# Score products of the global heads: 64-row operands for the keys' low parts, two heads at a time

## The chip, the cores and the metric

The kernel runs on one core of one Trainium2 chip. The metric is the device time of one execution in microseconds (us), as the median of several runs. The engines are named as in the profile: PE is the matrix engine's multiplying, PEld its loading of stationary operands ("weights"), DVE is VectorE, ACT is ScalarE, POOL is GpSimd, SP issues most of the transfers.

## The reference, cut to what matters

A two-layer encoder trunk on 1024 tokens of width 1024. Layer 0 projects its normalised input into three groups of heads and a gate; the group that matters here is the first, global attention with 8 query heads that share 2 key and value heads, of 64 channels each, every query against all 1024 keys:

```python
qa = rope_2d(rmsnorm(qa.reshape(B, S, A_HEADS, HEAD_DIM), q_norm_a[e]), grid_row, grid_col)
ka = rope_2d(rmsnorm(ka.reshape(B, S, A_KV, HEAD_DIM), k_norm_a[e]), grid_row, grid_col)
ya = global_gqa(qa, ka, va.reshape(B, S, A_KV, HEAD_DIM))
...
s = jnp.einsum('bqkgd,bskd->bkgqs', qblk, k).astype(jnp.float32) * scale
p = jax.nn.softmax(s, axis=-1).astype(v.dtype)
return jnp.einsum('bkgqs,bskd->bqkgd', p, v)
```

After it come windowed attention, attention over 256 memory tokens, a gate, an output projection, and layer 1 (neighbourhood attention). The change touches only the global attention of layer 0.

## The kernel before, in words

**Numbers in two parts.** Matrix products run on a 32-bit type that is multiplied at reduced precision (F32R). So nearly every operand is held as a high part and a low part (the value less its high part), and a product is the sum of high by high, high by low and low by high.

**Layout of the global heads.** Four pairs of heads (`even`, L1916, `for j in range(4)`), each done by one call of `global_pair` (L1024). For head `i` of a pair the tile `qs[i]` is 128 partitions by 1024 queries: the 64 rows from `64*i` on hold the queries' high parts, the other 64 rows their low parts (written so by `q_unit`, L917). The key tiles `kh` and `kl` hold the 64 channels of one key head twice, once on each half of the partitions: `kh` the high parts, `kl` the low parts. One 128-row product of `qs[i]` with `kh` thus gives high by high and low by high together; a second one, with `kl`, gives high by low, and low by low as well.

**One score** (`scores(i, g, b)`, L1030) takes one head `i` and 128 queries, block `2*g + b`. Four matrix products, each 128 rows by 128 queries by 512 keys, go to a PSUM tile `sa` of 128 by 1024 (two banks; there are two such tiles): for either half of the keys one with `kh` (L1035), then one with `kl` (L1036). DVE takes the maximum (L1040), ACT the exponential and its sum (L1041), DVE the reciprocal (L1042), POOL scales the result in the tile `P` (L1043). 16 scores make a pair; the order is all blocks of head 0, then all of head 1.

**Turning and multiplying.** For each head and each `g`, two blocks `P` are turned in 128 by 128 pieces (`flip`, L133), four to a PSUM tile `tr`; `p_parts` splits the result into a high part (ACT, L125) and a low part (DVE, L542), and each part is multiplied with the values `v` (L1068, 256 columns a product), over all keys, into the tile `o`. The values' high and low parts give the upper and the lower 64 rows of `o`; ACT copies the lower ones (`bt`, L1073), DVE adds the upper ones and writes 64 rows by 256 queries of the pair's output `y` (L1074).

**Work put between.** Projections of later tiles (gates, memory queries) are lists of steps of three 512-column products each (`token_steps`, L242). `pull(n)` issues `n` of them, and `issue_after` keeps them behind the newest score product or turn (`self.fence`). `global_pair` pulls 4 after each of its first two scores, then one at each pair of key blocks. Likewise one step of `side`, which makes sums of the output weights on POOL (`weight_sums`, L1246), follows each later score.

**What sets the order.** The program is written in this order and then put in another one by a scheduler that runs the instructions on a timeline of its own (`TC`, L52); the numbers of `AHEAD["l0"]` (L37) move a kind of instruction forward: `score` by 20, `exp` by 60, `part` by 150, `close` by 120. Each engine then runs its instructions in that fixed order.

**Buffers around it.** Tag `q` has 4 tiles, `P` 6, the PSUM tiles `sa` 2, `tr` 2, `o` 1. The `q` tiles of the next pair are loaded by L1021, and these can start only when the last score that reads a tile is done. After `global_pair`, `gated_rows` multiplies the whole `y` with its gate, and `mem_att` (L615) uses the `sa` tiles too.

Of the kernel before, what the change touches and what calls it, by code (L numbers as in the profile page):

```python
# [12 lines left out]
AF = mybir.ActivationFunctionType  # L13
OP = mybir.AluOpType
AX = mybir.AxisListType
# [3 lines left out]
T = 1024  # L19
# [45 lines left out]
class Trunk:  # L65
# [958 lines left out]
    def global_pair(self, qs, ks, v, kv, y, side):  # L1024

        nc = self.nc
        kh, kl = ks
        pts = {}

        def scores(i, g, b):  # L1030
            qb = qs[i][:, (2 * g + b) * 128:(2 * g + b + 1) * 128]
            s = self.ps("sa", (128, T))
            with self.ahead("score"):
                for c in range(0, T, 512):
                    nc.tensor.matmul(s[:, c:c + 512], qb, kh[:, c:c + 512], start=True, stop=False)  # L1035
                    self.fence = nc.tensor.matmul(s[:, c:c + 512], qb, kl[:, c:c + 512], start=False, stop=True)  # L1036
            st = self.tiny()
            pt = self.st("P", [128, T])
            with self.ahead("exp"):
                nc.vector.tensor_reduce(st[:, 0:1], s, axis=AX.X, op=OP.max, negate=True)  # L1040
                nc.scalar.activation(pt, s, AF.Exp, bias=st[:, 0:1], accum_out=st[:, 1:2])  # L1041
                nc.vector.reciprocal(st[:, 2:3], st[:, 1:2])  # L1042
                self.normal = nc.gpsimd.tensor_scalar(pt, pt, st[:, 2:3], 0.5, op0=OP.mult, op1=OP.mult)  # L1043
            pts[i, g, b] = pt

        todo = [(i, g, b) for i in range(2) for g in range(4) for b in range(2)]
        for _ in range(2):
            scores(*todo.pop(0))
            self.pull(4)
        for i in range(2):  # L1050
            for g in range(4):
                p = [pts[i, g, b] for b in range(2)]
                o = self.ps("pv")
                for c in range(0, 8, 2):
                    if c in (0, 4) and todo:
                        scores(*todo.pop(0))
                        with self.tc.issue_after(self.normal.ins):
                            next(side, None)
                    tr = self.ps("tr")
                    with self.ahead("flip"):  # L1060
                        self.flip((tr[:, (2 * k + b) * 128:(2 * k + b + 1) * 128],
                                   p[b][:, (c + k) * 128:(c + k + 1) * 128]) for k in range(2) for b in range(2))
                    parts = self.p_parts(tr, 512)
                    self.pull(1)
                    with self.ahead("pv"):
                        for k in range(2):
                            for part in parts:
                                nc.tensor.matmul(o[:, :256], v[:, c + k, kv, :], part[:, k * 256:(k + 1) * 256],  # L1068
                                                 start=(c + k == 0 and part is parts[0]),
                                                 stop=(c + k == 7 and part is parts[1]))  # L1070
                bt = self.st("bt", [64, 512])
                with self.ahead("close"):
                    self.copy(bt[:, :256], o[64:128, :256])  # L1073
                    nc.vector.tensor_tensor(y[64 * i:64 * i + 64, g * 256:(g + 1) * 256], o[0:64, :256], bt[:, :256],  # L1074
                                            op=OP.add)

# [1148 lines left out]
```

## Time and profile before

| what | value |
|---|---|
| median of 3 runs | 1484.51 us (1483.56 to 1491.91) |
| the profiled execution, its own time | 1488.39 us |
| its span, first to last instruction | 1486.6 us |
| share of the span in which PE, PEld, DVE, ACT, POOL were busy | 99%, 86%, 70%, 56%, 43% |
| first and last score product of the global heads | 144.3 us, 447.8 us |
| last output of the global heads (L1074) | 480.4 us |

The rows of a timeline give the start, the time taken, the engine, the line, the operation, output and inputs by tile names, the array's rows and columns that it uses ("128\*128"), and partitions by columns. Matrix products are pipelined: a product of 512 columns "takes" 0.39 us while the next one starts well before that is over, so the pace of PE is read from the starts and not from the durations. The table of groups has, behind the operation, the count, busy time, the mean of one in ns, and the idle time before it.

### The profile page before, as it was taken

What the parts mean: (1) busy time and instruction counts of PE and PEld (TensorE: products, weight loads), DVE (VectorE), ACT (ScalarE), POOL (GpSimd) and SP (SyncE); (2) the same over time, 40 slices, a digit from 0 to 9 for tenths busy, and PEclk for the clock granted to TensorE, in tenths of its full rate; (3) what the DMA queues carried; (4) which work ended last, traced back from release to release, by engine and by line L of the source; (5) the groups of instructions that cost most, each with busy time, mean ns of one, the idle gap of its engine ahead of it and who ended that gap; (6) DMA issues with size and microseconds to landing.
All of it is one profiled execution on the core that took longest, in us unless ns stands there. A gap on an engine that the chain in (4) does not pass through costs nothing.

```text
span 1486.6 us, 25518 instructions
## 1 busy us (share of the span) xinstructions
PE 1465.6 (99%) x8433; PEld 1275.1 (86%) x8433; DVE 1034.8 (70%) x2124; ACT 837.9 (56%) x1877; POOL 642.2 (43%) x767
## 2 busy tenths in 40 slices
PE   9899999999999999999999999999999999999998
PEld 8798888988888788888879887888998888888886
DVE  6687777777776578776687776654446787778674
ACT  7743665556655366655444444444446777777454
POOL 1223568556765656553450000001425556664454
PEclk9999999999999999999999999999999999999999
DMA  8966334334343524378553343567665568788834
GB/s 286 306 159 183 118 119 162 114 128 137 115 139 106 172 76 141 106 265 310 185 181 128 128 140 136 157 169 245 229 245 173 187 195 272 235 287 316 315 107 144
DMA packets 173860, 271.92 MB, mean 183 GB/s; under 512 B 15648, under 2 KB 96800, under 8 KB 172704
## 3 DMA queue, kind: packets, MB, share of 16 engines
q1 hardware_dynamic: 173296, 270.20, 56.2%
q8 instruction: 67, 1.10, 0.3%
q14 instruction: 65, 0.53, 0.1%
q10 hardware_dynamic: 432, 0.09, 0.0%
HBM read 174.28 MB, written 83.89 MB: 174 GB/s over the span
## 4 chain that ended last, share of the span: by engine, by line
PE 85%; DMA 5%; DVE 4%; issue 2%; ACT 2%; POOL 2%; SPq 0%; POOLq 0%; DVEq 0%; ACTq 0%
PE pj L242 15%; PE pj L62 11%; PE x L1619 7%; PE tr L133 6%; PE pv L1068 4%; PE y L1619 4%; PE pv L62 3%; PE s L62 3%; PE pj L1334 3%; PE tr L62 3%; PE sa L1334 2%; PE pv L1619 2%; PE sa L1035 2%; PE sa L1036 2%; PE s L1334 2%
## 5 line engine op out<-in xcount | busy, mean ns | idle before, releaser
L542 DVE TENSOR_TENSOR pl<-tr,ph 128x512 fp32r<-128x512 f32 (+2 forms) x352 | 204.1, 594 | 45.0 <-ACT ph L125 43.0
L242 PE MATMUL pj<-H,wh 128*128 128x512 f32 x704 | 233.7, 412 | 0.5 <-DVE vt L313 0.2
L125 ACT ACTIVATE ph<-tr 128x512 fp32r<-128x512 f32 (+2 forms) x352 | 176.3, 522 | 100.5 <-PE tr L133 76.4
L158 POOL TENSOR_SCALAR wh<-wraw 128x512 fp32r<-128x512 f32 x48 | 32.6, 682 | 275.9 <-PE x L1619 234.0
L125 ACT ACTIVATE wh<-wraw 128x384 fp32r<-128x384 f32 (+1 forms) x163 | 89.0, 553 | 99.4 <-DMA wraw<-w_mem 12.9
L242 PE MATMUL pj<-H,wl 128*128 128x512 f32 x352 | 139.1, 395 | 0.0
L242 PEld LDWEIGHTS pj<-H,wh 128*128 128x128 f32 x704 | 120.2, 189 | 18.3 <-POOL wh L158 1.1
L62 PE MATMUL pj<-H,wh 128*128 128x512 f32 x384 | 121.0, 396 | 0.0
L1121 POOL TENSOR_SCALAR pn<-pn,st 128x384 f32<-128x384 f32 (+1 forms) x128 | 72.4, 567 | 104.7 <-DVE st L1120 69.0
L133 PE MATMUL tr<-ident,P 128*128 128x128 f32 x752 | 115.4, 273 | 0.7 <-DVE pl L542 0.4
L1281 POOL TENSOR_TENSOR wl<-wraw,wh 128x384 fp32r<-128x384 f32 x56 | 63.2, 1130 | 91.4 <-ACT wh L125 85.6
L1119 ACT ACTIVATE pn<-pn,st 128x384 f32<-128x384 f32 (+1 forms) x128 | 75.1, 587 | 42.2 <-DVE st L1116 41.0
L133 PEld LDWEIGHTS tr<-ident,P 128*128 128x128 f32 x752 | 88.9, 140 | 9.1 <-DVE pl L542 1.4
L1041 ACT ACTIVATE P<-sa,st 128x1024 f32<-128x1024 f32 x64 | 71.5, 1117 | 35.3 <-PE tr L133 19.1
L1043 POOL TENSOR_SCALAR P<-P,st 128x1024 f32<-128x1024 f32 x64 | 74.0, 1159 | 32.3 <-DVE st L1042 32.3
L1040 DVE TENSOR_REDUCE st<-sa 128x1 f32<-128x1024 f32 x64 | 77.5, 1219 | 8.3 <-PE sa L1036 7.9
L62 PE MATMUL s<-k,q 128*128 128x384 f32 (+1 forms) x352 | 81.2, 327 | 0.0
L242 PEld LDWEIGHTS pj<-H,wl 128*128 128x128 f32 x352 | 66.2, 188 | 15.3
L62 PE MATMUL pj<-H,wl 128*128 128x512 f32 x192 | 75.6, 394 | 0.0
L160 POOL TENSOR_TENSOR wl<-wraw,wh 128x512 fp32r<-128x512 f32 x52 | 68.7, 1324 | 10.9 <-ACT wh L125 8.4
L62 PEld LDWEIGHTS pj<-H,wh 128*128 128x128 f32 x384 | 66.6, 188 | 5.4
L853 PE MATMUL pj<-ah,H 128*128 128x256 f32 x384 | 70.5, 281 | 0.0
(569 smaller groups left out, 4187.1 us busy)
## 6 DMA issues: line engine op xcount, KB each, us to landing
wraw<-w_o SPq DMA_DIRECT2D x52, 256.0 KB, 4.1
y<-yb SPq DMA_DIRECT2D x24, 512.0 KB, 3.2
wraw<-s SPq DMA_DIRECT2D x64, 192.0 KB, 3.7
wraw<-w_e SPq DMA_DIRECT2D x44, 256.0 KB, 3.2
k<-k SPq DMA_DIRECT2D x42, 256.0 KB, 5.4
s<-bias SPq DMA_DIRECT2D x56, 192.0 KB, 2.0
wq<-w_o SPq DMA_DIRECT2D x40, 256.0 KB, 3.4
y<-sg SPq DMA_DIRECT2D x18, 512.0 KB, 3.3
```

The costliest lines, as they stand in the source:

```text
L62: return lambda *a, **k: self.tc.keep_in_program_order(getattr(self.engine, name)(*a, **k))
L125: return self.nc.scalar.activation(out, in_, AF.Copy, scale=scale)
L133: self.turned = self.fence = self.pe.transpose(o, i, self.ident)
L242: self.pe.matmul(a[:, :n], s[:, kt % UNIT, :], m, start=(kt == 0 and i == 0), stop=(kt == KT - 1 and i == 2))
L542: self.low = nc.vector.tensor_tensor(pl[:, :n], tr[:, :n], ph[:, :n], op=OP.subtract)
L1040: nc.vector.tensor_reduce(st[:, 0:1], s, axis=AX.X, op=OP.max, negate=True)
L1041: nc.scalar.activation(pt, s, AF.Exp, bias=st[:, 0:1], accum_out=st[:, 1:2])
L1043: self.normal = nc.gpsimd.tensor_scalar(pt, pt, st[:, 2:3], 0.5, op0=OP.mult, op1=OP.mult)
L1119: nc.scalar.activation(o, o, AF.Exp, bias=st[:, 0:1], scale=-1.0, accum_out=st[:, 2:3])
L1121: self.normal = normal = nc.gpsimd.tensor_scalar(o, o, st[:, 3:4], 0.5, op0=OP.mult, op1=OP.mult)
L1334: last = nc.tensor.matmul(bank, s[:, k, :], y[3 * u + k][m][:, cols], start=start and u + k + e == 0, stop=u == 1 and k + e == 4, skip_gro ...
L1619: self.last = nc.tensor.matmul(bank, ws[s][:, k, :], b[k][m], start=start and k + i == 0, stop=k == UNIT - 1 and i == 2, skip_group_check= ...
```

## The change

The loop over scores of one head becomes a loop over blocks of queries, with both heads of the pair at once. For a block it takes both `sa` tiles and issues, in a fixed order (each product behind the one before it): four 128-row products with `kh` (head 1, then head 0, two halves of the keys each), then four products with `kl`, each of which uses only the 64 rows of the queries' high parts: rows 64 to 127 for head 1, rows 0 to 63 for head 0, in turn. The low-by-low part of the scores is no longer formed. The softmax of head 0 is written behind the products, that of head 1 two key-block pairs later (where before the next score stood). Turning and multiplying take the two heads of one block side by side, where they took two blocks of one head; the output's last addition, 64 rows by 256 queries, becomes two of 128 queries each, one for either head.

```diff
-        def scores(i, g, b):
-            qb = qs[i][:, (2 * g + b) * 128:(2 * g + b + 1) * 128]
-            s = self.ps("sa", (128, T))
+        def product(s, q, k, c, start):
+            with self.tc.issue_after(self.fence.ins) if self.fence else nullcontext():
+                self.fence = nc.tensor.matmul(s[:, c:c + 512], q, k[:, c:c + 512], start=start, stop=not start)
+
+        def scores(g, b):
+            qb = [q[:, (2 * g + b) * 128:(2 * g + b + 1) * 128] for q in qs]
+            ss = [self.ps("sa", (128, T)) for _ in range(2)]
             with self.ahead("score"):
+                self.fence = None
+                for i in (1, 0):
+                    for c in range(0, T, 512):
+                        product(ss[i], qb[i], kh, c, True)
                 for c in range(0, T, 512):
-                    nc.tensor.matmul(s[:, c:c + 512], qb, kh[:, c:c + 512], start=True, stop=False)
-                    self.fence = nc.tensor.matmul(s[:, c:c + 512], qb, kl[:, c:c + 512], start=False, stop=True)
...
+                    for i in (1, 0):
+                        r = slice(64 * i, 64 * i + 64)
+                        product(ss[i], qb[i][r], kl[r], c, False)
+            for i, s in enumerate(ss):
...
+                pts[i, g, b] = pt
+                yield
+
+        def sided():
+            with self.tc.issue_after(self.normal.ins):
+                next(side, None)
+        todo = [(g, b) for g in range(4) for b in range(2)]
+        for _ in scores(*todo[0]):
             self.pull(4)
...
+        for n, (g, b) in enumerate(todo):
+            p = [pts[i, g, b] for i in range(2)]
+            o = self.ps("pv")
+            later = scores(*todo[n + 1]) if n + 1 < len(todo) else None
+            for c in range(0, 8, 2):
+                if c in (0, 4) and later:
+                    next(later)
+                    sided()
...
+                for i in range(2):
+                    nc.vector.tensor_tensor(y[64 * i:64 * i + 64, (2 * g + b) * 128:(2 * g + b + 1) * 128],
+                                            o[0:64, i * 128:(i + 1) * 128], bt[:, i * 128:(i + 1) * 128], op=OP.add)
```

More of the change, by code (lines that the diff above doesn't have):

```diff
@@ L1033, in scores @@
             with self.ahead("score"):
+                self.fence = None
+                for i in (1, 0):
+                    for c in range(0, T, 512):
+                        product(ss[i], qb[i], kh, c, True)
                 for c in range(0, T, 512):
-                    nc.tensor.matmul(s[:, c:c + 512], qb, kh[:, c:c + 512], start=True, stop=False)
-                    self.fence = nc.tensor.matmul(s[:, c:c + 512], qb, kl[:, c:c + 512], start=False, stop=True)
-            st = self.tiny()
@@ L1038, in scores @@
[L1038 to L1046, printed above, removed]
@@ L1047, in global_pair @@
-        for _ in range(2):
-            scores(*todo.pop(0))
-            self.pull(4)
[L1050 to L1075, printed above, removed]
```

22 lines of the change are left out of this document (added).

## The prediction

> **What bounds the kernel now.** I read the page first: PE is busy in 99% of the span, so the question is what PE pays for. Then the busy time by stretches from 140 to 460 us, in which all score products of the global heads lie (only the first and the last stretch and the sum are shown; the columns are the engines' busy us and counts, then the granted clock, the DMA share and GB/s), and the waits of PE in the same window.
>
> ```profile
> span 1486.6 us, 25518 instructions
> PE 1465.6 (99%) x8433; PEld 1275.1 (86%) x8433; DVE 1034.8 (70%) x2124; ACT 837.9 (56%) x1877; POOL 642.2 (43%) x767
> ```
> ```profile
> 140.00:180.00 40.00, 39.91 (x221) 33.92 (x220) 28.95 (x45) 22.93 (x40) 27.96 (x31) 1.00 0.44 128
> ...
> 420.00:460.00 40.00, 40.00 (x261) 36.00 (x261) 30.36 (x49) 22.60 (x44) 27.18 (x35) 1.00 0.37 111
> sum 320.00, PE 319.52 PEld 280.52 DVE 234.59 ACT 190.38 POOL 209.31; mean PE 39.94 PEld 35.06 DVE 29.32 ACT 23.80 POOL 26.16
> ```
> ```profile
> PE tr L133 <- DVE pl L542: 0.4, 1, 0.4
> ```
>
> PE works through 319.52 of 320 us, waits once for 0.4 us, and its clock is full (1.00). The next engine, DVE, is busy 234.59 us, 73%. So here a microsecond of PE is a microsecond of the kernel, until something else falls due. The chain of waits says the same, and the table of groups gives the counts:
>
> ```profile
> by line: PE pj L242 39.2%; PE tr L133 18.0%; PE pv L1068 17.1%; PE sa L1035 9.2%; PE sa L1036 9.2%; PE pv L670 2.6%; PE sa L630 1.2%; PE sa L629 1.2%; PE sa L631 1.2%; DVE sg L438 0.5%; DVE vt L313 0.2%; ACT sg L437 0.2%; DVE pl L542 0.2%;
> ```
> ```profile
> L1035 PE MATMUL sa<-k,q 128*128 128x512 f32 x128 | 51.6, 403 | 0.0
> L1036 PE MATMUL sa<-k,q 128*128 128x512 f32 x128 | 50.2, 392 | 0.0
> ```
>
> The products with the low key parts (L1036) are 9.2% of 320 us, 29.4 us. The pace of one comes from the timeline of PE in a run of them, and that of the weight loads from the same stretch of PEld:
>
> ```profile
> 252.16 0.39 PE L1035 MATMUL sa<-k,q 128*128 128x512 f32 x1
> 252.39 0.40 PE L1036 MATMUL sa<-k,q 128*128 128x512 f32 x1
> ...
> 253.32 0.39 PE L1036 MATMUL sa<-k,q 128*128 128x512 f32 x1
> 253.55 0.28 PE L1068 MATMUL pv<-ph,va 128*128 128x256 f32 x1
> ```
> ```profile
> 252.16 0.19 PEld L1036 LDWEIGHTS sa<-k,q 128*128 128x128 f32 x1
> 252.40 0.19 PEld L1035 LDWEIGHTS sa<-k,q 128*128 128x128 f32 x1
> ```
>
> From 252.16 to 253.55 there are six steps, so 0.232 us each; 128 of them are 29.7 us, which agrees with the chain. A product lives 0.39 us, 0.16 us longer than until the next one starts. The load for a product starts at the moment its predecessor starts (252.16, 252.40): PE loads one product ahead.
>
> **The change part by part.**
>
> *The paired products.* All 256 score products stay; 128 of them shrink from 128 rows to 64, and neighbours use opposite halves of the array. Every product in the trace has the form 128\*128, so no row shows whether two halves run at once. Bounds: not at all, 0; wholly, a pair in the time of one, which saves 2 x 0.232 = 0.464 us for a block of queries (four products with `kl`) and, with 32 blocks, 14.8 us. Two loads have to fit in each 0.232 us. That they can is seen where products follow faster than loads are needed here:
>
> ```profile
> 257.12 0.46 PEld L133 LDWEIGHTS tr<-ident,P 128*128 128x128 f32 x4
> 257.55 0.19 PEld L1035 LDWEIGHTS sa<-k,q 128*128 128x128 f32 x1
> 257.66 0.19 PEld L1036 LDWEIGHTS sa<-k,q 128*128 128x128 f32 x1
> ```
> ```profile
> 257.22 0.60 PE L133 MATMUL tr<-ident,P 128*128 128x128 f32 x4
> 257.58 0.47 PE L1035 MATMUL sa<-k,q 128*128 128x512 f32 x1
> 257.89 0.39 PE L1036 MATMUL sa<-k,q 128*128 128x512 f32 x1
> ```
>
> Loads start 0.11 us apart (257.55, 257.66), so two take 0.22 us. I take the pairs as running together.
>
> *The second load of a pair.* PE loads one product ahead, so at the first pair the second half's weights are loaded only once the first half runs. The rows above price a product without weights ready: from 257.58 to 257.89 are 0.31 us in place of 0.232, 0.08 us too many. From then on both halves stay offset by that much. Bounds 0 and 0.11 us (one load) a block; I take 0.08.
> The Trainium skill (TensorE: Matmul & The Clock Gate, Part 3 on packing small matmuls) gives about 4 ns between the starts of products in different row groups. By it this term is nothing and the sum below would be -7.2 us instead of -4.6; no run here shows it yet.
>
> *The two edges of a block.* PE goes from 128-row products to 64-row ones and back: 64 edges in all. The trace has no such change. Nearest below: from the turns (32-bit, 128 columns) to the products of L1035, where PE also changes what it does, only the missing load shows, 0.08 us. Bounds: 0 if the edge is free; 0.35 us if the array must empty (0.16, the life of a product beyond its successor's start) and then load in full (0.19). Between them: the empty array plus an uncovered load as the rows show it, 0.16 + 0.08 = 0.24. I take half of that, 0.12 us, since nothing in the rows says that all products must be out before the next may enter.
>
> *Sum for PE.* A block: 0.464 - 0.08 - 2 x 0.12 = 0.144 us gained; 32 blocks: 4.6 us.
>
> *Softmax of two heads at once.* The counts of L1040 to L1043 are as before. Both `sa` tiles are now filled together and both must be empty before the next block, where before one was read while the other was filled:
>
> ```profile
> L1040 DVE TENSOR_REDUCE st<-sa 128x1 f32<-128x1024 f32 x64 | 77.5, 1219 | 8.3 <-PE sa L1036 7.9
> L1042 DVE RECIPROCAL st<-st 128x1 f32<-128x1 f32 x64 | 10.1, 158 | 24.8 <-ACT P L1041 24.5
> L1074 DVE TENSOR_TENSOR yb<-pv,bt 64x256 f32<-64x256 f32 x29 | 11.9, 412 | 2.0 <-ACT bt L125 1.5
> ```
> ```profile
> L1041 ACT ACTIVATE P<-sa,st 128x1024 f32<-128x1024 f32 x64 | 71.5, 1117 | 35.3 <-PE tr L133 19.1 <-DVE st L1040 16.1
> L1041 ACT ACTIVATION_READ_ACCUMULATOR P<-sa,st 128x1 f32 x64 | 12.6, 197 | 0.0
> ```
> ```profile
> L1043 POOL TENSOR_SCALAR P<-P,st 128x1024 f32<-128x1024 f32 x64 | 74.0, 1159 | 32.3 <-DVE st L1042 32.3
> ```
>
> Two maxima, one exponential and its sum: 2 x 1.219 + 1.117 + 0.197 = 3.75 us from a block's last product until both tiles are free; with the reciprocal and the scaling 0.158 + 1.159 = 5.07 us until the second `P` is ready. Blocks are 10.5 us apart on average (336.1 us, from the first score product at 144.3 to the last output at 480.4, over 32):
>
> ```profile
> L1035 PE MATMUL sa<-k,q x128: 388/393/486, 144.3 to 447.6; 128*128 128x512 f32 x128
> ```
> ```profile
> L1074 DVE TENSOR_TENSOR yb<-pv,bt x32: 397/418/420, 165.9 to 480.4; 64x256 f32<-64x256 f32 x32
> ```
>
> Each pair's first block has 8 pulled steps of 0.70 us (172.39 to 173.09 below) behind it, 5.6 us, which covers 5.07. So I price it at nothing; what hides it is the turning, the value products and the pulled steps. Without that cover it is the third rival.
>
> *The output's addition.* 32 additions of 64x256 (0.412 us) become 64 of 64x128. Bounds: the same total, or twice, 13.2 us more on DVE. DVE would go from 73% to 77% at most; PE hides it, so nothing. On the last block of a pair the gate waits up to 0.4 us longer, with the memory attention's products on PE meanwhile.
>
> *What else moves.* Pulled steps and `side` steps are as many as before (8 and 32; 14 a pair), behind the newest score as before. Both heads' `q` tiles are now held until a pair's last block, where the first came free at half; so the two loads for the next pair, on SP's queue with the projection weights behind them, can start later than they did. The rows of their issue and landing, and of the first pair's last score and the second pair's first:
>
> ```profile
> L1021 SPq DMA_DIRECT2D q<-qa x6: 320/430/590, 166.5 to 368.4; - x6
> ...
> DMA to landing us min/median/max: 3.6/4.8/6.0
> ```
> ```profile
> 192.07 0.40 PE L1035 MATMUL sa<-k,q 128*128 128x512 f32 x1
> ```
> ```profile
> 214.29 0.39 PE L1035 MATMUL sa<-k,q 128*128 128x512 f32 x1
> ```
>
> 22 us lie between, and a load lands in 6.0 at most. Nothing.
>
> *Sum.* -4.6 us. The profiled execution took 1488.4 us, 1.8 beyond its span and 3.9 over the median; the products cost the same in each, so I subtract from the median: 1484.5 - 4.6 = **1479.9 us**.
>
> **The rivals.**
>
> *Free edges, 1469.7 us.* The halves run together, offset and edges cost nothing: the whole 14.8 us. For it: loads run one product ahead, and a change from turns to products costs no more than its load. Against it: a different use of the rows of the array is more than another operation.
>
> *The array empties at both edges, 1487.6 us: slower than before.* Place: between the last product with `kh` and the first with `kl`, and between the last with `kl` and whatever follows. Price 0.24 us each: 0.464 - 0.08 - 0.48 = -0.096 a block, +3.1 us. It decides from 0.192 us an edge on, where 0.464 - 0.08 is used up. For it: products overlap by 0.16 us and each block has two edges for only two saved steps. Against it: no row shows PE emptying itself by its own will. Should the loads not be overlapped either (0.35 us an edge, 0.11 us offset), it is +11.1 us, 1495.6.
> The Trainium skill states this rule (TensorEngine Tiling (Array Packing), Key Properties): a change of the tiling mode, unlike a change of tile, drains TensorE. Its cost in time is not given there, and no run here has shown it so far.
>
> *Both score tiles are late, 1488.9 us.* Where scores follow closely, a pair of them comes every 4.96 us:
>
> ```profile
> 170.55 0.40 PE L1035 MATMUL sa<-k,q 128*128 128x512 f32 x1
> ...
> 172.39 0.62 PE L242 MATMUL pj<-H,wh 128*128 128x512 f32 x2
> ...
> 173.09 0.40 PE L1035 MATMUL sa<-k,q 128*128 128x512 f32 x1
> ...
> 175.51 0.39 PE L1035 MATMUL sa<-k,q 128*128 128x512 f32 x1
> ```
>
> A block at that pace, 4.82 us with the gain, has 1.71 us of products (8 x 0.232 - 0.144), which leaves 3.11 us for 3.75 us of softmax: PE waits 0.64 us. Over half of the 28 later blocks that is 9.0 us, +4.4 in all; over all of them +13.3. Against it: the average distance of 10.5 us, and an order that is made with such waits in view.
>
> *The halves run one after the other, 1492.2 us.* A 64-row product then costs the same 0.232 us and the edges stay: 64 x 0.12 = +7.7 us (1506.9 at 0.35 an edge). The change would not do what it says. The trace says nothing for or against it except that loads would not stop it.
>
> **How the numbers follow.** Forecast 0.38, free edges 0.17, emptied array 0.20, late score tiles 0.15, one after the other 0.10. The range goes from 1467, the free case less 2.7 us for a luckier order of the rest (PE idles only 1486.6 - 1465.6 = 21 us in all, so there is little to win), to 1494, beyond the last rival and just short of the bound of 1495.6. The forecast's own range is 1474 to 1484. A measurement of this kernel tells about 1% from no change, 14.8 us: that is what the free case just reaches, so faster by more gets 0.11 (half of that case and a little for order), slower by more 0.08 (products in turn with full edges, or late tiles at every block), and within 1% the rest, 0.81.
>
> **What would show it.** Right: 128 products of form 64\*128 in the stage; the second of a pair starts about 0.1 us behind the first and the next pair 0.23 us after that one; 0.3 to 0.4 us instead of 0.232 from the last 128-row product to the first 64-row one, and the same on the way out; PE still at 99% and its stage some 5 us shorter. Wrong: 64-row products 0.232 us apart (one after the other); gaps of 0.45 us and more at the edges (emptied); PE idle before L1035's successors, released by ACT's exponential (late tiles); a stage 15 us shorter (free).

## The result and the profile after

The changed kernel takes 1492.87 us (median of 20 runs), the kernel before 1486.7 us (median of 20 runs, a little over the 1484.51 us of its first three). The ratio is 1.0041, with a 95% interval of 1.0031 to 1.0051: slower by 6.1 us, 4.6 to 7.6. One of the changed kernel's 20 runs took 5093 us; nothing recorded says why, and the ratio leaves it out. The forecast was 1479.9 us.

The page of the changed kernel, its span and busy times:

```profile
span 1490.8 us, 25565 instructions
PE 1467.1 (98%) x8433; PEld 1257.3 (84%) x8433; DVE 1039.8 (70%) x2156; ACT 839.6 (56%) x1877; POOL 649.0 (44%) x767
```

The table of groups by form, from 140 to 460 us of the changed kernel, score products and the output's addition (count, busy us, mean ns, idle us before):

```profile
L1032 PE MATMUL sa<-k,q 128*128 128x512 f32 x128 | 40.7, 401 | 3.5 <-ACT P L1051 3.3
L1032 PE MATMUL sa<-k,q 64*128 64x512 f32 x128 | 25.2, 446 | 0.0
```
```profile
L1087 DVE TENSOR_TENSOR yb<-pv,bt 64x128 f32<-64x128 f32 x58 | 16.2, 280 | 3.7 <-ACT bt L125 3.2
```

The change did what it says: 128 products of form 64\*128. Their busy time is 0.62 of the others' (25.2 against 40.7 us, though each lives a little longer), because two of them run at once. But PE, which before waited once for 0.4 us, now waits 3.3 us for ACT's exponential.

How long the stage with the global heads takes can be read from two rows that neither kernel changes: the last turn before it (L133 with `rp`) and the first score of the window heads behind it (L699). First the kernel before, then the changed one (min, median and max ns of one, first and last start in us):

```profile
L133 PE MATMUL tr<-ident,rp x40: 270/272/328, 61.8 to 144.0; 128*128 128x128 f32 x40
...
L699 PE MATMUL sa<-k,q x64: 277/338/442, 501.7 to 644.8; 128*128 128x384 f32 x48, 128*128 128x256 f32 x16
```
```profile
L133 PE MATMUL tr<-ident,rp x40: 270/273/327, 58.7 to 141.5; 128*128 128x128 f32 x40
...
L699 PE MATMUL sa<-k,q x64: 277/338/445, 504.9 to 647.7; 128*128 128x384 f32 x48, 128*128 128x256 f32 x16
```

From 144.0 to 501.7 were 357.7 us; from 141.5 to 504.9 are 363.4 us. The stage is 5.7 us longer, so nearly the whole 6.1 us lies in it. (The two profiled spans differ by 4.2 us only: the changed kernel's execution reached the stage 2.5 us earlier, in a part that the change doesn't touch. So the stage is compared, and not the span.) The same two rows give the "stage" of each experiment below. The busy times by stretches show where PE stands: first the kernel before, then the changed one, the stretch from 300 to 340 us and the sum from 140 to 500.

```profile
300.00:340.00 40.00, 40.00 (x223) 34.06 (x222) 28.96 (x42) 23.90 (x46) 22.47 (x28) 1.00 0.38 125
...
sum 360.00, PE 359.34 PEld 314.08 DVE 259.10 ACT 211.28 POOL 231.69; mean PE 39.93 PEld 34.90 DVE 28.79 ACT 23.48 POOL 25.74
```
```profile
300.00:340.00 40.00, 37.43 (x189) 28.08 (x188) 24.26 (x38) 18.88 (x35) 21.56 (x23) 1.00 0.33 112
...
sum 360.00, PE 355.64 PEld 292.69 DVE 260.32 ACT 211.34 POOL 232.99; mean PE 39.52 PEld 32.52 DVE 28.92 ACT 23.48 POOL 25.89
```

PE is idle 4.36 us of 360 where it was idle 0.66, and 2.57 of these lie in one stretch, where the third pair of heads begins. The clock is full in both.

**A block that runs as written.** The timeline of PE in the changed kernel, and below it that of the weight loads. A row merges neighbours of one line, shows the form of the first of them, and its time runs to the end of the last:

```profile
261.38 0.62 PE L1032 MATMUL sa<-k,q 128*128 128x512 f32 x2
261.92 0.73 PE L1032 MATMUL sa<-k,q 64*128 64x512 f32 x4
262.59 0.39 PE L1080 MATMUL pv<-pl,va 128*128 128x256 f32 x1
262.81 0.28 PE L1080 MATMUL pv<-ph,va 128*128 128x256 f32 x1
```
```profile
261.14 0.42 PEld L1032 LDWEIGHTS sa<-k,q 128*128 128x128 f32 x2
261.92 0.30 PEld L1032 LDWEIGHTS sa<-k,q 64*128 64x128 f32 x4 [0.36 <-issue]
262.59 0.19 PEld L1080 LDWEIGHTS pv<-pl,va 128*128 128x128 f32 x1 [0.37 <-DVE pl L542]
```

Four 64-row products take 0.67 us, from 261.92 to the next product at 262.59, where four 128-row ones took 0.93 in the kernel before. The single records put the starts at 261.375, 261.606 (128 rows), 261.924 and 261.928 (first pair), 262.262 and 262.265 (second pair), 262.589: the halves of a pair start 3 to 4 ns apart. Their loads begin at 261.92, with the pair and not before it, and the next product's load begins at 262.59, with that product. So the loading ahead stops at each change of form. Over the 30 blocks that run so, the means are: 0.320 us from the last 128-row product to the pair, 0.336 from pair to pair, 0.327 (without the very first block) to the product behind, and 0.32 or 0.22 instead of 0.232 or 0.12 for the step after that one, where it is a product of 512 or 256 columns (in 11 of the 30 blocks it is a turn, and there the step is longer by some 0.06). Against steps of 0.232 us this makes 0.09 + 0.10 going in and 0.10 + 0.10 coming out: 0.39 us for one way in and out, of 0.464 saved. A block gains 0.07 us, these 30 together about 2.1.

**The blocks that don't.** At the third pair's start the scheduler set pulled steps between the low products. The timeline of PE there:

```profile
310.49 1.08 PE L1032 MATMUL sa<-k,q 128*128 128x512 f32 x4
311.50 0.49 PE L1032 MATMUL sa<-k,q 64*128 64x512 f32 x1
311.93 0.49 PE L242 MATMUL pj<-H,wh 128*128 128x512 f32 x1
312.35 0.50 PE L1032 MATMUL sa<-k,q 64*128 64x512 f32 x1
...
314.06 0.49 PE L1032 MATMUL sa<-k,q 64*128 64x512 f32 x1
...
315.76 0.40 PE L670 MATMUL pv<-pl,mk 128*128 128x512 f32 x1
317.17 0.74 PE L1032 MATMUL sa<-k,q 128*128 128x512 f32 x2 [1.01 <-ACT P L1051]
...
327.60 0.74 PE L1032 MATMUL sa<-k,q 128*128 128x512 f32 x2 [1.20 <-ACT P L1051]
```

From 311.50 on each step is an edge: 0.42 us instead of 0.232, seven times up to 314.48, 1.3 us; with the first way in and the load behind the last one it is 1.5. Two blocks later, at 331.7, one of the four low products was left behind three value products, for 0.5 us more by the same reckoning. And PE stands at 317.17 and at 327.60, for the tile that the softmax still reads. The engines of that softmax, DVE and ACT, in the same timeline:

```profile
314.59 2.36 DVE L1050 TENSOR_REDUCE st<-sa 128x1 f32<-128x1024 f32 x2 [4.17 <-PE sa L1032]
...
315.91 1.11 ACT L1051 ACTIVATE P<-sa,st 128x1024 f32<-128x1024 f32 x1 [1.15 <-DVE st L1050]
```

The last low product starts at 314.06, the maxima at 314.59, the first exponential ends at 317.02, and PE goes on at 317.17: 3.1 us behind the block's last product. All waits of PE from 141 to 503 us in the changed kernel (total us, times, longest):

```profile
PE sa L1032 <- ACT P L1051: 3.3, 5, 1.2
PE pv L1080 <- ACT ph L125: 0.4, 1, 0.4
PE pj L242 <- POOL wh L158: 0.3, 1, 0.3
PE pj L242 <- DVE vt L331: 0.2, 1, 0.2
```

A wait's idle time understates it: the product before the one at 317.17 starts at 315.76, so this step is 1.41 us where 0.232 was due, though only 1.01 us of it count as idle. Counted by the starts, the five steps that end in a wait for the exponential are 4.3 us longer than the steps of the kernel before. The weights of the next product are late then too (they load from 317.28 on, with the first of the two already running), 0.10 us each time. That is 4.8 of the 5.7 us by which the stage is longer; PE's short waits, counted in the same way, make 0.9 us more than in the kernel before, and so the pairs come out near nothing.

From the starts of the 256 products one can also read why. From a block's last product to the first one of the next lie 3.1 to 3.7 us in 21 of 31 cases, and 3.1 us is what the freeing of the first tile took above. Two products of the next block (the high ones of one head) are put that early, in 29 of the 32 blocks 1.5 to 6 us ahead of the other six; presumably the scheduler's own timeline has a tile free there, which no run shows. So there is hardly any slack between the exponential and these products, however far the blocks' other products are apart.

### The profile page after: what moved, and what is told of

It reads as the page before. It is cut to its first block, busy times and chain, and to the rows that moved or that the text cites. A ratio compares the mean times of both kernels' runs of the same rounds, so it can differ in the third digit from the quotient of the medians.

```text
span 1490.8 us, 25565 instructions
## 1 busy us (share of the span) xinstructions
PE 1467.1 (98%) x8433; PEld 1257.3 (84%) x8433; DVE 1039.8 (70%) x2156; ACT 839.6 (56%) x1877; POOL 649.0 (44%) x767
## 4 chain that ended last, share of the span: by engine, by line
PE 83%; DMA 5%; DVE 4%; ACT 2%; issue 2%; POOL 2%; SPq 1%; POOLq 0%; DVEq 0%; ACTq 0%
PE pj L242 14%; PE pj L62 11%; PE x L1632 7%; PE tr L133 6%; PE pv L1080 4%; PE y L1632 4%; PE sa L1032 3%; PE pv L62 3%; PE s L62 3%; PE pj L1347 3%; PE sa L1347 2%; PE tr L62 2%; PE pv L1632 2%; PE s L1347 2%; PE tr L1347 2%
## 5 line engine op out<-in xcount | busy, mean ns | idle before, releaser
L242 PEld LDWEIGHTS pj<-H,wh 128*128 128x128 f32 x704 | 120.1, 190 | 18.8 <-POOL wl L160 0.7
L133 PE MATMUL tr<-ident,P 128*128 128x128 f32 x752 | 116.4, 274 | 0.5 <-POOL P L721 0.2
L133 PEld LDWEIGHTS tr<-ident,P 128*128 128x128 f32 x752 | 88.4, 140 | 12.6 <-DVE pl L542 2.6
L1053 POOL TENSOR_SCALAR P<-P,st 128x1024 f32<-128x1024 f32 x64 | 78.3, 1230 | 22.6 <-DVE st L1052 21.8
```

What stands on the lines that cost most here:

```text
L133: self.turned = self.fence = self.pe.transpose(o, i, self.ident)
L242: self.pe.matmul(a[:, :n], s[:, kt % UNIT, :], m, start=(kt == 0 and i == 0), stop=(kt == KT - 1 and i == 2))
```

## The experiments

The theories, numbered as in the expectations: 1, the edges cost what the unbroken blocks show, and what is lost beyond them is the broken block with the waits behind it (the low products of one block set apart); a rival to it for the edges is the array that empties, at 0.24 us an edge. 2, the edges eat up the saving in every block. 3, the rearrangement alone (both heads at once) costs some 6 us, whatever the rows. This was then parted into 4, the two score tiles that are filled together, and 5, the rest of the rearrangement (turning two heads side by side, the addition in two parts). Each ratio is to runs of the kernel before from the same session: 1488.12 us for the first four experiments, 1488.57 for the next four, 1486.36 for the last three.

**full_rows: the changed order with the low products on 128 rows.** The order on all engines is that of the changed kernel.

```diff
-                        r = slice(64 * i, 64 * i + 64)
-                        product(ss[i], qb[i][r], kl[r], c, False)
+                        product(ss[i], qb[i], kl, c, False)
```

> The changed kernel with one part undone: the low products use all 128 rows again; the order on every engine stays exactly that of the changed kernel. Theory 1 (the pairs run as forecast and save some 0.07 us a block; the loss sits in one place, the start of the third pair, where the low products of a block alternate with pulled projection steps, so eight edges in place of two, and the next blocks then wait for the score tiles): this kernel regains the 5.1 us of that place and gives up 31 x 0.07 = 2.2 us, so about 3 us under the changed kernel and 2 to 4 us over the one before (0.15 to 0.25%). Theory 2 (the edges eat the saving in every block and more): equal to the kernel before within 1 us. Theory 3 (taking both heads at once costs, by late score tiles, whatever the rows): not faster than the changed kernel, 5 us or more over the one before.

Measured: 1494.33 us, ratio 1.0040 (1.0025 to 1.0055). The same as the changed kernel, so without any 64-row product and without any edge the time is just as far above the kernel before. Theory 2, which expected the time of the kernel before, falls, and theory 1 as the only cause; theory 3 has the size. The largest of PE's waits from 141 to 503 us:

```profile
PE sa L1032 <- ACT P L1050: 3.4, 5, 1.2
PE pv L1079 <- DVE pl L542: 0.6, 1, 0.6
PE tr L133 <- DVE pl L542: 0.6, 2, 0.4
PE pv L1079 <- ACT ph L125: 0.4, 1, 0.4
```

The first line is the same five waits for the exponential, in the same places. The stage of the profiled execution is 367.2 us (141.3 to 508.5), 9.5 over the kernel before. Of these, 4.9 are the waits for the exponential, counted by the starts as above, and about 1.7 are a stretch of lower clock right behind the two long waits (last section).

**contig: the changed kernel with the low products held together.**

```diff
-                for c in range(0, T, 512):
-                    for i in (1, 0):
-                        r = slice(64 * i, 64 * i + 64)
-                        product(ss[i], qb[i][r], kl[r], c, False)
+                with self.tc.high_priority(400):
+                    for c in range(0, T, 512):
+                        for i in (1, 0):
+                            r = slice(64 * i, 64 * i + 64)
+                            product(ss[i], qb[i][r], kl[r], c, False)
```

> The changed kernel with the low products moved further forward in the scheduler's order (by 400 instructions), so that nothing comes between them; this changes 20 lines of the order on TensorE, all at the start of the third pair, and none on another engine. Theory 1: 4 to 5 us under the changed kernel, 0 to 1.5 us over the one before (ratio 1.000 to 1.001). Theories 2 and 3: within 1 us of the changed kernel, ratio about 1.004.

Measured: 1489.58 us, ratio 1.0012 (1.0000 to 1.0024); stage 360.9 us (143.7 to 504.6). All 32 blocks now run unbroken. Against the changed kernel's ratio that is 0.0029 less, 4.3 us; by the stages it is 2.5 us. The profile accounts for the smaller figure: 2.0 us of edges, and 0.6 of the wait at the third pair's start. Theory 1 is right in kind about this part; its size is somewhere between the two. The five waits for the exponential remain, with a smaller sum and the same longest:

```profile
PE sa L1032 <- ACT P L1052: 2.7, 5, 1.2
```

**four_edges: two pairs of edges per block.**

```diff
-                for i in (1, 0):
-                    for c in range(0, T, 512):
-                        product(ss[i], qb[i], kh, c, True)
                 for c in range(0, T, 512):
-                    for i in (1, 0):
-                        r = slice(64 * i, 64 * i + 64)
-                        product(ss[i], qb[i][r], kl[r], c, False)
+                    with self.tc.high_priority(400 if c else 0):
+                        for i in (1, 0):
+                            product(ss[i], qb[i], kh, c, True)
+                    with self.tc.high_priority(400):
+                        for i in (1, 0):
+                            r = slice(64 * i, 64 * i + 64)
+                            product(ss[i], qb[i][r], kl[r], c, False)
```

> The kernel with unbroken low products, but for each half of the keys in turn: two products with the high parts, then the pair with the low parts. So each block changes form four times in place of two; the pairs are the same. If an edge costs what the changed kernel's timeline shows (0.086 us on the way in, 0.092 on the way out, and 0.10 less for two pairs that no longer follow each other): 0.076 us a block, 2.4 us over the kernel with unbroken low products. If the array empties at each edge at 0.24 us: 32 x (2 x 0.24 - 0.10) = 12 us over it.

Measured: 1502.13 us, ratio 1.0096 (1.0073 to 1.0120), 12.5 us over contig; stage 374.9 us (140.9 to 515.8), 14.0 over. That is the sum that I had expected of the emptied array (12), and not my 2.4 us. The loads of its weights show what I had left out:

```profile
164.75 0.18 PEld L1032 LDWEIGHTS sa<-k,q 64*128 64x128 f32 x2 [0.37 <-issue]
165.19 0.30 PEld L1032 LDWEIGHTS sa<-k,q 128*128 128x128 f32 x2 [0.25 <-issue]
165.85 0.19 PEld L1032 LDWEIGHTS sa<-k,q 64*128 64x128 f32 x2 [0.37 <-issue]
166.28 0.19 PEld L1081 LDWEIGHTS pv<-ph,va 128*128 128x128 f32 x1 [0.25 <-issue]
```

A load starts with its product at each edge, so these rows give the steps too: 0.44 us for a single pair to the product behind it (164.75 to 165.19), two 128-row products in 0.66 (165.19 to 165.85), 0.43 for the second pair (165.85 to 166.28). Together 1.53 us, where four steps of 0.232 and nothing more would be 0.93. One more way in and out thus costs 12.5 / 32 = 0.39 us (0.44 by the stages), about the 0.39 that the single block above gave once the uncovered load behind it is counted. So the sum of the emptied array came out without its price of 0.24 us an edge being shown. I had read only the steps into and out of the pairs, and missed the late load of the step after.

**half_alone: the kernel before, its low products on 64 rows, one head at a time.**

```diff
                 for c in range(0, T, 512):
-                    nc.tensor.matmul(s[:, c:c + 512], qb, kh[:, c:c + 512], start=True, stop=False)
-                    self.fence = nc.tensor.matmul(s[:, c:c + 512], qb, kl[:, c:c + 512], start=False, stop=True)
+                    self.fence = nc.tensor.matmul(s[:, c:c + 512], qb, kh[:, c:c + 512], start=True, stop=False)
+                r = slice(64 * i, 64 * i + 64)
+                for c in range(0, T, 512):
+                    with self.tc.high_priority(400), self.tc.issue_after(self.fence.ins):
+                        self.fence = nc.tensor.matmul(s[:, c:c + 512], qb[r], kl[r, c:c + 512], start=False, stop=True)
```

> The kernel before with one part of the change alone: the low products use the 64 rows of the queries' high parts, both halves of the keys one after the other, but one head at a time, so no product has a partner on the other half of the array. If 64 rows without a partner cost as much as 128 and the edges what the changed kernel shows (0.086 in, 0.092 out, 0.107 for the late second load behind it): 64 x 0.2 to 0.29 = 13 to 18 us over the kernel before. If a 64-row product were itself cheaper, or the edges free: equal to the kernel before or below it.

Measured: 1508.48 us, ratio 1.0141 (1.0114 to 1.0168), 20.4 us over the kernel before, somewhat over what I expected; stage 381.4 us (141.5 to 522.9). PE's timeline, two scores in a row:

```profile
248.82 0.71 PE L1035 MATMUL sa<-k,q 128*128 128x512 f32 x2
249.46 0.73 PE L1039 MATMUL sa<-k,q 64*128 64x512 f32 x2
250.11 0.74 PE L1035 MATMUL sa<-k,q 128*128 128x512 f32 x2
```

A 64-row product without a partner saves nothing: two of them take 0.65 us from the first to the next 128-row product, more than the 0.464 of two 128-row ones. 20.4 us over 64 scores is 0.32 us a score, and 0.37 by the stage (23.7 us): a way in and out without any gain.

**one_tile: the rearrangement without the two tiles.** `scores` is that of the kernel before again, one score after the other, each with its own tile and four 128-row products, as before; but the order is both heads of a block, turned and multiplied side by side, with the addition in two parts.

```diff
-        todo = [(g, b) for g in range(4) for b in range(2)]
-        for _ in scores(*todo[0]):
+        todo = [(i, g, b) for g in range(4) for b in range(2) for i in range(2)]
+        for _ in range(2):
+            scores(*todo.pop(0))
             self.pull(4)
...
-                if c in (0, 4) and later:
-                    next(later)
+                if c in (0, 4) and todo:
+                    scores(*todo.pop(0))
                     sided()
```

> The rearrangement without the pairs and without two score tiles at once: one score at a time with 128 rows, as before, but the heads of a pair in turn, turned and multiplied side by side, with the output's addition in two parts. Its order on TensorE differs from the kernel before in 3 lines. The 128-row version of the changed kernel stayed as slow as the changed kernel (ratio 1.004), so the rearrangement costs some 6 us. Theory 4 (that cost is the two score tiles that are filled together: TensorE stands before the first product of a block until the exponential of the block before has freed a tile): equal to the kernel before within 1.5 us (0.1%). Theory 5 (turning the heads together, the additions in two parts or the q tiles that are held longer cost it): 4 us or more over it.

Measured: 1485.81 us, ratio 0.9987 (0.9975 to 0.9998); stage 357.4 us (141.1 to 498.5), against 357.7. So theory 5 falls: turning the two heads side by side and adding in two parts costs nothing that these runs show. It is the only kernel of the study at or below the time before, by 0.13%. PE's waits from 141 to 503 us, the whole list:

```profile
PE tr L133 <- DVE vt L311: 0.2, 1, 0.2
PE pj L242 <- DVE vt L331: 0.2, 1, 0.2
```

What full_rows has beyond one_tile is the two tiles filled together, with the order on PE that follows from it, and 0.0053 in the ratio, 7.9 us; the two intervals are far apart.

**fenced: the eight products in one run.** If the first two products of a block stand too early, they can be tied to the rest: contig without the line that frees the first product from the newest fence.

```diff
             with self.ahead("score"):
-                self.fence = None
                 for i in (1, 0):
```

> The kernel with unbroken low products, and the first product of a block kept behind the newest turns in TensorE's order (the chain is no longer cut at its start). In the scheduler's order 26 of 32 blocks become eight products in a row, where two of them used to stand 10 to 40 instructions ahead of the other six. Theory 4: the waits before the two early products, 5.2 us in the kernel with unbroken low products (1.6 + 2.1 + 0.9 + 0.6), mostly go; 2 to 5 us under that kernel, so 0 to 3 us under the kernel before (ratio 0.998 to 1.000). If the block as a whole now waits for the second tile instead: no faster than that kernel (1.001).

Measured: 1505.51 us, ratio 1.0119 (1.0104 to 1.0133); stage 376.5 us (142.3 to 518.8). My expectation failed by some 16 us; neither of its branches had such a loss. The waits for the exponential shrink, and another one appears:

```profile
PE pj L242 <- DVE vt L313: 7.0, 11, 1.0
PE sa L1032 <- ACT P L1051: 1.2, 3, 0.4
```

L313 is DVE's reader of the projections' tile `pj`. The timelines of DVE and PE at one of the three longest waits show what keeps it:

```profile
241.25 2.36 DVE L1050 TENSOR_REDUCE st<-sa 128x1 f32<-128x1024 f32 x2 [2.71 <-PE sa L1032]
243.52 0.68 DVE L313 TENSOR_TENSOR vt<-pj,rows 128x512 f32<-128x512 f32 x1
...
244.25 0.73 PE L242 MATMUL pj<-H,wh 128*128 128x512 f32 x2 [1.00 <-DVE vt L313]
```

With two tiles complete at once, two maxima stand in a row on DVE, 2.36 us, the reader of `pj` behind them, and PE behind that. So part of the waiting moved from the tile `sa` to the tile `pj`, and the root there is the same: two softmaxes fall due at one time. PE is idle for 11.7 of the stage's 376.5 us; what else makes it 18.8 us longer was not followed up.

**late2f and late2f_full: the products moved by two key blocks.** fenced, with the next block's products written at key blocks 2 and 6 instead of 0 and 4; the second of the two with 128 rows.

```diff
-                if c in (0, 4) and later:
+                if c in (2, 6) and later:
                     next(later)
```

> As the kernel with the chain not cut, but a block's products are written one pair of key blocks later, so behind later turns: 30 of 32 blocks are eight products in a row. Theory 4: as that kernel or up to 1 us better, ratio to before 0.997 to 1.000. If the softmax, now later, makes the turns of the next block wait: slower than that kernel by the waits of TensorE on POOL or DVE, ratio 1.002 or more.

> The kernel with the products written later, with 128 rows for the low products in place of 64; the order on every engine is the same. It gives what the pairs alone are worth when little waits: a block with pairs is 0.464 us shorter, less 0.09 us drain and 0.10 us uncovered load at the way in and 0.09 and 0.107 at the way out, so 0.07 to 0.08 us (0.18 where a 512-column product follows, which covers the load): 32 blocks, 2.5 to 4 us over the kernel with 64 rows. If the edges cost as much as the pairs save, equal within 1 us; if the array emptied and loaded in full (0.35 us an edge), 7 us or more under it.

Measured: 1500.76 us, ratio 1.0092 (1.0077 to 1.0107), and 1502.65 us, ratio 1.0103 (1.0086 to 1.0120); stages 370.9 us (143.9 to 514.8) and 372.1 us (141.3 to 513.4). In the first one PE waits for the scaling on POOL, presumably since the second `P` is now due sooner:

```profile
PE tr L133 <- POOL P L1053: 2.8, 6, 1.4
```

All the listed waits of late2f make only 5.2 of the 13.2 us by which its stage is longer; another 18 steps to a value product end in a wait for DVE's low part that is too short for the list, about 0.2 us each.

The two differ by the 64 rows alone, 1.9 us in the medians, a little under what I expected, and their intervals overlap. It agrees with the 0.07 us a block, some 2.3 us for 32, of the steps and doesn't prove it.

**before_half, full_rows_half, contig_half: a shorter softmax.** If the wait is for the softmax, a shorter one must take the loss away. In all three the maximum is taken over half of the columns, so half of that work is left out and the result is no softmax any more; the exponential is replaced by a hyperbolic tangent over the same columns.

```diff
-                    nc.vector.tensor_reduce(st[:, 0:1], s, axis=AX.X, op=OP.max, negate=True)
-                    nc.scalar.activation(pt, s, AF.Exp, bias=st[:, 0:1], accum_out=st[:, 1:2])
+                    nc.vector.tensor_reduce(st[:, 0:1], s[:, 0:512], axis=AX.X, op=OP.max, negate=True)
+                    nc.scalar.activation(pt, s, AF.Tanh, bias=st[:, 0:1], accum_out=st[:, 1:2])
```

> A measure for the next two: the kernel before with the maximum of a score taken over 512 of its 1024 columns (so it leaves out half of that work and the softmax is not the reference's; the exponential is a hyperbolic tangent of the same shape, to keep the numbers bounded). A maximum takes some 0.6 us in place of 1.22. TensorE is the bound in this stage and hardly waits, so all theories expect the kernel before within 1.5 us (0.1%).

> The 128-row version of the changed kernel with the same half of the maximum left out and the same tangent. Theory 4 (the loss comes from both softmaxes falling due at once: two maxima, 2.4 us in a row, on VectorE, and 3.75 us until both score tiles are free): the burst shrinks by 1.2 us, about the length of the single waits seen (0.5 to 1.4 us each), so the 6 us over the kernel before shrink to 2 or less over the kernel before with half the maximum. Theory 5 (another part of the rearrangement): still 5 us or more over it.

> The kernel with unbroken low products of 64 rows, with the same half of the maximum left out and the same tangent. Theory 4: what is left is what the pairs save net of their edges, 0.07 to 0.1 us a block: 1 to 4 us under the kernel before with half the maximum, and 2 to 4 us under the 128-row version with half the maximum. If the pairs save nothing net of their edges: equal to that version within 1 us. Theory 5: some 2 us over the kernel before, as without this.

Measured: before_half 1490.66 us, ratio 1.0030 (1.0011 to 1.0050), though its stage is 356.9 us (140.8 to 497.7) and I had expected no difference; full_rows_half 1491.15 us, 1.0032 (1.0021 to 1.0044); contig_half 1488.29 us, 1.0016 (1.0005 to 1.0027). The clearest figure is the waiting. PE's waits for the exponential fall from 3.4 us (five) in full_rows to 1.7 (two) in full_rows_half, and from 2.7 (five) in contig to 0.6 (one) in contig_half, from 141 to 503 us:

```profile
PE sa L1032 <- ACT P L1052: 0.6, 1, 0.6
```

So these waits follow the length of the softmax, as theory 4 has it. The times say less. By the medians the two tiles cost only 0.5 us with a shorter softmax (full_rows_half against before_half), where they cost 6.2 with the full one, but this rests on before_half, which is itself 4.3 us over the kernel before. Its profiled execution (1485.97 us) is the fastest of its ten, so no trace shows where these 4.3 us lie. Against the kernel before, full_rows_half is still 4.8 us slower. contig_half, where the pairs run unbroken, is 2.9 us under full_rows_half, as expected of the pairs, with intervals that overlap. Its profiled stage is 365.3 us (141.2 to 506.5), 8.4 over before_half. The waits in it, of which the first is for a tile of the memory attention:

```profile
PE tr L133 <- POOL P L655: 2.1, 1, 2.1
PE sa L1032 <- ACT P L1050: 1.7, 2, 1.0
```

About 1.7 us more of it are a stretch of lower clock. So this triple supports theory 4 by its waits and leaves the times open.

**The tally.** The two tiles at once cost about 6.0 us (full_rows, 0.0040; 7.9 against one_tile). In the changed kernel's order the pairs give back little of it: 2.1 us by the unbroken blocks' steps, from which the two broken blocks' edges take 2.0. That makes 5.9 us, with 6.1 measured (4.6 to 7.6). With the blocks held together (contig) 1.8 us of loss remain, 0.0012 of 1488.12, with an interval from 0 to 3.6. The same tally, 6.0 less 2.3, would leave 3.7, and contig's profiled stage is 3.2 us longer than that of the kernel before. So the medians don't close to better than 2 us.

## Why the prediction was wrong, point by point

The result lies in the range (1467 to 1494) and not on the forecast's side: it was one of the rivals.

**The bound.** Right: PE is the bound, and what PE waits for is what the kernel loses.

**Paired products, 0.464 us a block.** Right: the halves run wholly together.

**"The second load of a pair", 0.08 us.** Wrong as put: the halves start 3 to 4 ns apart, not 0.1 us. A late load of 0.10 us is there all the same, for the first pair as a whole. So the term came near the right size by luck.
The Trainium skill (TensorE: Matmul & The Clock Gate, Part 3 on packing small matmuls) gives about 4 ns for the halves, and the trace agrees: 3 to 4 ns. The same part says that loads for other row groups, or for the spare weight buffer, are drawn ahead of running products. At the changes of form no trace here shows that: the pair's loads start at 261.92, with the pair.

**"The two edges of a block", 0.12 us each.** Mis-sized. Going in costs 0.09 us and the load of 0.10 just named, coming out 0.10 us and a second uncovered load of 0.10. Edges and load together were priced at 0.32 us a block, and measure 0.39. The sum was 4.6 us and is 2.3 for 32 unbroken blocks: a part of the miss, and not the one that turned the sign.
The rival of the emptied array ("0.24 us each") had 0.56 us a block with its late load, 0.17 too many: it used up all of the gain, and the unbroken blocks keep 0.07 us. Its 0.24 us an edge (0.16 for the emptying, 0.08 for the load) measure 0.19 to 0.20 (0.09 to 0.10 for the step, 0.10 for the load), and its 0.08 us for the second load are one of these loads over again.
The Trainium skill (TensorEngine Tiling (Array Packing), Key Properties) has it that a change of the tiling mode drains TensorE. The trace fits that with a delay of 0.09 to 0.10 us on each side, besides the load that isn't drawn ahead, but doesn't show an empty array: by its modelled ends the last 128-row product of the block above is done at 261.99, and the pair starts at 261.92.

**"Softmax of two heads at once ... I price it at nothing".** This is the step that failed, and it turned the sign: the waits for the exponential that it left out are 4.8 us in the changed kernel's profile, and the two tiles cost 6.0 us in full_rows. I put 5.07 us of softmax under an average distance of 10.5 us. But the next block's first products don't come 10.5 us later; the order has them 3.1 to 3.7 us behind the last product of the block before, in 21 of 31 cases, which is just when the first tile comes free (3.1 us in the case above). An average over the stage said nothing about that gap. The rows to ask were those of the gap itself, and the third rival had one of them.

**The rival "both score tiles are late", 1488.9 us.** This one came true, with its sign, at ratio 1.0041 instead of 1.0030. Its price was 0.64 us at half of 28 blocks, 9.0 us; there are five waits of up to 1.2 us, 3.3 us of idle time and 4.8 by the starts. It also took off the forecast's 4.6 us of gain, of which next to nothing is left in the changed kernel. Too high a price for the waits and too high a gain partly cancel, so that its total came close is partly luck. That the order "is made with such waits in view" was no protection: the waits are there all the same.

**Not foreseen.** The chain that holds the eight products in order doesn't hold them together: the scheduler put other products between the low ones of two blocks. It costs 2.0 us in edges, and contig, where they are held together, is 4.3 us faster by the medians and 2.5 by the stages.

**The output's addition, the `q` tiles.** Right at nothing: 64 additions of 0.28 us are 18 us where 32 of 0.412 were 13, and one_tile, which has the additions in two parts too, is not slower. No wait for a `q` tile of these heads is among PE's.

**The other rivals.** Free edges: refuted by the steps. One after the other: refuted by the starts.

## What to carry to other kernels

Half-array products among full ones have to earn their way in and out: here it costs 0.39 us, as much as 1.7 full products, so a run of two pairs, which saves 2.0 products, comes out almost even. Longer runs should pay better by this sum; none was tried. Check also what a grouping does to the engines that read the result: what is filled together falls due together, and the gap to compare with the reader's time is that from the last product of a group to the first one that needs its buffer again, not the average distance. And where a scheduler makes the order, look at the first products that it moves forward, and at what it puts between products that belong together.

## What the runs showed of the hardware

Weight loads start one product ahead in an unbroken run of products of one form, and with their own product at each change between 128-row and 64-row form, in both directions. At every such change in the stages of the changed kernel, contig, four_edges and half_alone the load and its product start within 0.03 us of each other.

In two of the profiled executions the clock fell for a short while behind long waits of PE. In full_rows, right after those at the third pair's start, the busy times by stretches (the third figure from the right is the granted clock):

```profile
320.00:330.00 10.00, 8.44 (x37) 6.57 (x36) 5.52 (x9) 3.79 (x7) 3.79 (x4) 0.93 0.28 105
330.00:340.00 10.00, 10.00 (x59) 8.76 (x58) 5.90 (x10) 4.96 (x9) 7.94 (x10) 0.90 0.33 93
```

It was halved for 3.4 us, from 328.6 to 332.0, which costs about 1.7 us. The same came in full_rows_half from 221.2 to 224.6 us, behind a stretch in which PE was busy for 7.68 of 10 us. The changed kernel, with equally long waits, keeps its full clock over the same stretch, so what decides on it stays open, and none of the 5.7 us of its stage is such a stretch. How often one falls into the other executions of full_rows is not known, since each kernel has but one profiled execution.
